# Attention block on one core: the lower part of V accumulated into the columns of its upper part

## The chip, the cores and the metric

The kernel runs on one core of one Trainium2 chip. The metric is the device time of one execution in microseconds (us); lower is better. Three timed runs of the kernel before gave 1442.44, 1429.75 and 1431.9 us, median 1431.9 us. A further execution was profiled, and all rows below come from it.

## The reference, cut to what matters

One block of a transformer: T = 1024 tokens, width 1024, a mixed attention of 8 dilated-window heads ("A") and 8 sparse heads in two groups ("B"), then an output projection and an MLP of width 4096. The change touches the place where probabilities meet V, in both halves:

```python
# A: three dilated windows, mixed by their denominators
e = jnp.where(mask, jnp.exp(s - m[..., None]), 0.0)
den = jnp.sum(e, axis=-1)
o = jnp.einsum('bhrnqk,bhrnkd->bhrnqd', e, vb.astype(jnp.float32)) / den[..., None]
...
# B: a selected and a sliding-window branch, gated and added to a compressed one
p_sel = masked_softmax(ss, (kpos <= tpos[:, None])[:, :, None])
o_sel = jnp.einsum('bgrqk,bgqkd->bgrqd', p_sel, vg.astype(f32))
...
p_win = masked_softmax(sw, wmask)
o_win = jnp.einsum('bgrqk,bgkd->bgrqd', p_win, vw.astype(f32))
out = gb[..., 0:1] * o_cmp + gb[..., 1:2] * o_sel + gb[..., 2:3] * o_win
...
h_res = h_res + mixed @ w_out[l]
h = rms_norm(h_res, norm_mlp[l])
h_res = h_res + jnp.square(jax.nn.relu(h @ w_up[l])) @ w_down[l]
```

## The kernel before, in words

Every float32 product is made of parts: a value is split into an upper part (a rounded copy) and a lower part (the rest), and upper times upper, upper times lower and lower times upper are summed in PSUM. The matmuls of projections, scores, output projection and MLP do so in fp32r. The product of probabilities and V does so in float16.

**V.** A tile of V has 130 float16 columns for each head and each block of 128 keys (L216). `split_v` (L200) puts the upper part into columns 64 to 127 and the lower part into columns 0 to 63; column 128 holds ones (L217) and yields the softmax denominator.

**One unit of attention** is one block of 128 queries, one head, and n blocks of 128 keys. `attend` (L503) runs it in steps:

- `st_scores` (L400): TensorE makes the scores (L417, L419, in B also a mask product, L421), VectorE adds mask or table and takes the extreme of a row (L428), for some units GpSimd adds a constant to that extreme (L432), ScalarE takes the exponential (L433).
- `st_trans` (L435): ScalarE writes the upper part of the probabilities in float16 (L447), GpSimd (L449) or VectorE (L451) writes the lower part, by turns D, P, P; one transposing DMA on SyncE's queue (L452) turns both into `pt`, with keys on the partitions. Units of at most 4 key blocks go through this step in pairs of two heads.
- `st_pv` (L457): for each key block t two matmuls. L467 takes the upper probabilities as weights and streams 129 columns of V (lower, upper, ones); L468 takes the lower probabilities as weights and streams 65 (upper, ones), added to columns 64 to 128. So a unit's result stands in PSUM as [product with V's lower part, 64 | all other products, 64 | denominator, 1]. Two heads lie side by side in one tile of tag `O`, 2 x 129 = 258 columns, and are evicted together after the second.

A unit's product is held back: it is issued one unit later in A (`DEPA`), three in B (`DEPB`).

**Eviction and the halves.** In A, VectorE copies the first 64 columns of both heads into `oaw` (L477), adds the next 64 from PSUM (L478), and copies the denominators (L479). When the four query blocks of a pair of heads are done, `done` (L609) divides (GpSimd, L613) and stores `oaw` to DRAM by SyncE's queue (L614). There is one buffer `oaw`, and while the A units run there is one PSUM bank of tag `O` (`nbank`, L342); from the second half of B's preparation on there are two. In B, ScalarE copies all 258 columns into the tile `ot` (L473, a tile of 8 heads x 129). After the eighth head `b_done` (L832) follows: VectorE scales and inverts the denominators (L835, L836), GpSimd multiplies them by the gate (L837), adds the two halves (L838), multiplies by the gated inverse (L839) and adds to the other branches (L840). After the second branch of a block, `finalize` (L845) squares the sum on ScalarE (L848, which writes its unneeded squares into columns 64 to 127 of `ot`) for the norm.

**Order of the work.** The list `P1` (L28) sets A's four pairs of heads, the projections and the compression of keys in turn, with projection matmuls between A's units. B then runs the query blocks in the order 5, 7, 6, 4, 3, 2, 1, 0 (`ORD`), the sliding window ahead of the selected blocks, with pieces of the output projection (L705) put in by a credit (`pump`, L857) and later jobs by a count (`waiting`). The MLP follows (L1042 ff.). The program is built by a framework that orders instructions by priority and a simulated timeline when it compiles, so each engine's order is fixed in the program; on the chip each engine runs its own list in order and waits on semaphores.

Of the kernel before, what the change touches and what calls it, by code (L numbers as in the profile page):

```python
# [9 lines left out]
F32 = mybir.dt.float32  # L10
# [3 lines left out]
AF = mybir.ActivationFunctionType  # L14
OP = mybir.AluOpType
# [41 lines left out]
def build(tc, A, out):  # L57
# [3 lines left out]
    pe, act, dve, pool, sp = nc.tensor, nc.scalar, nc.vector, nc.gpsimd, nc.sync  # L61
# [93 lines left out]
    vsc = cst.tile([128, 4], F32, name="vsc")  # L155
# [168 lines left out]
    oad = tc.dram_tile([NT, 128, 512], F32, name="oad")  # L324
# [21 lines left out]
    def bank(tag, shape, bufs=None):  # L346
        if tag == "F" and nbank[pst["second"]]["F"] == 0:
            tag = "O"
        n = nbank[pst["second"]][tag]
        p = pst["pool"] if tag in "OF" else psp  # L350
        t = p.tile([128, 512], F32, name=tag, tag=tag, bufs=n)
        if len(shape) == 3:
            return t[:, :shape[1] * shape[2]].rearrange("p (a b) -> p a b", a=shape[1])
        return t[:, :shape[1]]
# [7 lines left out]
    def k_stacks(ke, ko, srcs):  # L362
        n = len(srcs)
        ps = transposes(srcs)
        for e, o, i in zip(KS, (ke[0:64], ko[64:128]), (0, 64)):
            if e == "A":
                act.activation(o, ps[i:i + 64, :n], AF.Copy)
            else:
                dve.tensor_copy(o, ps[i:i + 64, :n])
        dve.tensor_sub(ke[64:128], ps[0:64, :n], f32(ke[0:64]))  # L370
        dve.tensor_sub(ko[0:64], ps[64:128, :n], f32(ko[64:128]))

    def q_stacks(qe, qo, q2, srcs):
        n = len(srcs)
        ps = transposes(srcs)
        for e, o, i in zip(QS, (qe[0:64], qo[64:128], qe[64:128], qo[0:64]), (0, 64, 0, 64)):
            if e == "A":
                act.activation(o, ps[i:i + 64, :n], AF.Copy, scale=0.125)
            else:
                dve.tensor_scalar(o, ps[i:i + 64, :n], 0.125, None, op0=OP.mult)  # L380
        dve.scalar_tensor_tensor(q2[0:64, 0], ps[0:64, :n], 0.125, f32(qe[0:64]), op0=OP.mult, op1=OP.subtract)
        dve.scalar_tensor_tensor(q2[64:128, 1], ps[64:128, :n], 0.125, f32(qo[64:128]), op0=OP.mult, op1=OP.subtract)
# [74 lines left out]
    def st_pv(u):  # L457
        n = u["n"]
        e = u["e"]
        if e == 0:  # L460
            OP2[0] = bank("O", [128, 258]).rearrange("p (a b) -> p a b", a=2)
        pss = OP2[0]
        ps = pss[:, e]
        for t in range(n):
            v = u["v"](t)
            ph, pl = u["pt"][t]
            pe.matmul(ps, ph, v[:, 0:129], start=t == 0, stop=False)  # L467
            pe.matmul(ps[:, 64:129], pl, v[:, 64:129], start=False, stop=t == n - 1)  # L468
        if e == 0:
            return  # L470
        if "ev" in u:
            if EV[u["h"] // 2] == "A":
                act.activation(u["ev"], pss, AF.Copy)  # L473
            else:
                dve.tensor_copy(u["ev"], pss)
        else:
            dve.tensor_copy(u["out"], pss[:, :, :64])  # L477
            dve.tensor_add(u["out"], u["out"], pss[:, :, 64:128])  # L478
            dve.tensor_copy(u["den"], pss[:, :, 128:129])  # L479

    OP2 = [None]
    pend = []
# [20 lines left out]
    def attend(u):  # L503
        st_scores(u)
        if paired(u) and not u["e"]:
            first[0] = u
        else:
            us = [first[0], u] if paired(u) else [u]
            st_trans(us)
            pend.append(us)  # L510
            retire(DEPB if "i" in u else DEPA)
        for job in waiting:
            job[0] -= 1
        due = [job for job in waiting if job[0] <= 0]
        waiting[:] = [job for job in waiting if job[0] > 0]
        for job in due:
            with later(0):
                pinned(u, job[1])
        if "i" in u:
            pump(u)  # L520
# [76 lines left out]
    def a_pair(hp):  # L597
        c = ("qk", hp)
        st = ST[c]
        k = asp.tile([128, 2, NT, 128], F32R, name="ak", bufs=1)  # L600
        for a in (0, 4):
            k_stacks(k[:, 0, a:a + 4], k[:, 1, a:a + 4], [st[:, t, 128:256] for t in range(a, a + 4)])
        for a in (4, 0):
            oaw = asp.tile([128, 4, 2, 64], F32, name="oaw", bufs=1)
            den = asp.tile([128, 4, 2], F32, name="dena", bufs=2)
            q = asp.tile([128, 2, 4, 128], F32R, name="aq", bufs=2)
            q2 = aq2
            q_stacks(q[:, 0], q[:, 1], q2, [st[:, t, 0:128] for t in range(a, a + 4)])
            def done(den=den, oaw=oaw, a=a):  # L609
                dve.tensor_scalar(den, den, vsc[:, hp // 2:hp // 2 + 1], None, op0=OP.mult)  # L610
                dve.reciprocal(den, den)
                o3 = oaw.rearrange("p t e d -> p (t e) d")
                pool.tensor_mul(o3, o3, den.rearrange("p t e -> p (t e)")[:, :, None].to_broadcast([128, 8, 64]))  # L613
                sp.dma_start(oad[a:a + 4, :, hp * 128:(hp + 1) * 128].rearrange("t p c -> p t c"),  # L614
                             oaw.rearrange("p t e d -> p t (e d)"))

            for i in range(3, -1, -1):
                for e in range(2):
                    u = dict(q=q[:, e, i], q2=q2[:, e, i], k=k[:, e].rearrange("p a b -> p (a b)"),
                             n=a + i + 1, tab=la[:, (7 - a - i) * 128:],  # L620
                             v=lambda t, e=e: V["a", hp][:, t, e], den=den[:, i, :, None], out=oaw[:, i], e=e)
                    if i == 0 and e == 1:
                        u["done"] = done
                    attend(u)
# [12 lines left out]
    ssm = cst.tile([128, 2, NT], F32, name="ssm")  # L637
# [82 lines left out]
    QB, OC, SB, OT, OB, DEN = {}, {}, {}, {}, {}, {}  # L720
# [3 lines left out]
    def fb(i, shape, dt, name, bufs):  # L724
        if name in FB:
            n = fbn[name] = fbn.get(name, -1) + 1
            if n % bufs == 0:
                return bqp.tile(shape, dt, name=name + "0", bufs=1)
            bufs -= 1
        return bpp.tile(shape, dt, name=name, bufs=bufs)  # L730
# [75 lines left out]
    def b_attend(i, br):  # L806
        n0 = max(0, i - 4)
        if br == 0:
            OB[i] = wop.tile([128, 8, 64], F32, name="ob", bufs=3)

        def f(br, h):
            g, j = divmod(h, 4)
            q, q2 = QB[i]
            if h == 0:
                OT[i, br] = fb(i, [128, 8, 129], F32, "ot", 2)
            k = kb[br][:, g].rearrange("p a b -> p (a b)")
            a, n = (0, i + 1) if br == 0 else (n0, i + 1 - n0)
            u = dict(i=i, h=h, q=q[:, g, j], q2=q2[:, g, j], k=k[:, a * 128:], n=n,
                     v=lambda t: V["kw" if br else "ks"][:, a + t, g], ev=OT[i, br][:, h - 1:h + 1], e=h % 2)
            if br:  # L820
                u["tab"] = wint[:, (5 - n) * 128:]
            else:
                u["sc"] = SB[i, g]
            return u

        for h in range(8):
            u = f(br, h)
            if h == 7:
                u["done"] = lambda: b_done(i, br)
            attend(u)  # L830

    def b_done(i, br):  # L832
        o = OT[i, br]
        d = DEN[i, br] = cst.tile([128, 8], F32, name="den", bufs=4)
        dve.tensor_scalar(d, o[:, :, 128], vsc[:, 2 + br:3 + br], None, op0=OP.mult)  # L835
        dve.reciprocal(d, d)  # L836
        pool.tensor_mul(d, d, gate[:, i].rearrange("p (h b) -> p b h", b=3)[:, 1 + br])  # L837
        pool.tensor_add(o[:, :, 0:64], o[:, :, 0:64], o[:, :, 64:128])  # L838
        pool.tensor_mul(o[:, :, 0:64], o[:, :, 0:64], d[:, :, None].to_broadcast([128, 8, 64]))  # L839
        pool.tensor_add(OC[i] if br else OB[i], o[:, :, 0:64], OC[i])  # L840
        if br == 0:
            finalize(i)
# [2 lines left out]

    def finalize(i):
        fin.add(i)
        act.activation(OT[i, 0][:, :, 64:128], OB[i], AF.Square, accum_out=ssm[:, 1, i:i + 1])  # L848
        rms_of(rmm[:, 1, i:i + 1], ssm[:, 1, i:i + 1], 512)

    pieces = []
# [240 lines left out]
    ps = [bank(x, [128, 512]) for x in "OF"]  # L1092
# [124 lines left out]
```

## Time and profile before

| | us |
|---|---|
| median of three runs | 1431.9 (1429.75 to 1442.44) |
| the profiled execution | 1436.43 |
| its span, first to last instruction | 1434.6 |
| TensorE matmul busy | 1356.6 (95%), 8267 matmuls |
| VectorE, ScalarE, GpSimd busy | 804.2, 620.4, 512.7 |
| mean granted TensorE clock | 0.976 of full |
| first and last product with V (L467, start) | 83.6 and 698.3 |

How to read the rows: PE is TensorE's matmuls, PEld its weight loads, DVE is VectorE, ACT ScalarE, POOL GpSimd, SP SyncE. "out<-in" names the tiles written and read. Matmuls are pipelined, so the duration of one (0.19 to 0.23 us for the products with V) is longer than its distance to the next; distances are read from the starts. In the table by windows each engine has its busy time in that stretch with the number of its instructions; after them come the granted clock, the busy share of the 16 DMA engines and the data rate. In the list of waits stands who waited for whom, the total, the number of times, and the longest. In the groups, "| 21.1, 1405 | 5.9 <-..." is busy time in us, mean of one in ns, and the engine's idle time just before the group with what ended it.

### The profile page before, as it was taken

What the parts mean: (1) busy time and instruction counts of PE and PEld (TensorE: products, weight loads), DVE (VectorE), ACT (ScalarE), POOL (GpSimd) and SP (SyncE); (2) the same over time, 40 slices, a digit from 0 to 9 for tenths busy, and PEclk for the clock granted to TensorE, in tenths of its full rate; (3) what the DMA queues carried; (4) which work ended last, traced back from release to release, by engine and by line L of the source; (5) the groups of instructions that cost most, each with busy time, mean ns of one, the idle gap of its engine ahead of it and who ended that gap; (6) DMA issues with size and microseconds to landing.
All of it is one profiled execution on the core that took longest, in us unless ns stands there. A gap on an engine that the chain in (4) does not pass through costs nothing.

```text
span 1434.6 us, 21829 instructions
## 1 busy us (share of the span) xinstructions
PE 1356.6 (95%) x8267; PEld 1150.8 (80%) x8267; DVE 804.2 (56%) x1728; ACT 620.4 (43%) x1092; POOL 512.7 (36%) x728
## 2 busy tenths in 40 slices
PE   8999999998978999899899999999999999999997
PEld 6898889998966777678678888888888888888886
DVE  6674656673467887877454434443354344443436
ACT  6572746763567777776472112211212112122115
POOL 3445564574466566877411111111111111111114
PEclk9999999999899999899999999999999999999998
DMA  5265563975558987765431111111112111111002
GB/s 186 67 127 132 100 139 70 227 153 135 93 148 167 159 155 138 141 118 103 111 111 30 59 45 59 46 41 47 45 59 59 44 30 46 58 59 45 1 0 118
DMA packets 285193, 131.55 MB, mean 92 GB/s; under 512 B 219040, under 2 KB 272288, under 8 KB 285088
## 3 DMA queue, kind: packets, MB, share of 16 engines
q1 hardware_dynamic: 284944, 129.90, 39.5%
q8 instruction: 65, 1.06, 0.3%
q14 instruction: 40, 0.33, 0.1%
q10 hardware_dynamic: 144, 0.26, 0.0%
HBM read 68.26 MB, written 8.39 MB: 53 GB/s over the span
## 4 chain that ended last, share of the span: by engine, by line
PE 65%; POOL 7%; DVE 7%; DMA 7%; issue 4%; ACT 4%; SPq 0%; POOLq 0%; DVEq 0%; ACTq 0%
PE dn L1056 8%; PE dn L1058 8%; PE dn L1057 8%; PE up L1024 8%; PE up L1022 8%; PE up L1023 8%; DMA pt<-hl 2%; PE F L334 2%; PE F L335 2%; PE F L336 2%; PE T L359 1%; DVE ns L428 1%; PE S L417 1%; POOL hl L449 1%; DMA pt<-hlx 1%
## 5 line engine op out<-in xcount | busy, mean ns | idle before, releaser
L1033 POOL TENSOR_TENSOR ul<-ua,uh 128x512 fp32r<-128x512 f32 x64 | 83.6, 1306 | 607.2 <-ACT uh L1032 527.7
L1059 DVE SCALAR_TENSOR_TENSOR st<-dn,r2q,st 128x512 f32<-128x512 f32 (+1 forms) x257 | 191.5, 746 | 155.9 <-PE dn L1058 152.4
L1056 PE MATMUL dn<-wdh,uh 128*128 128x512 f32 (+1 forms) x514 | 203.1, 395 | 0.0
L1058 PE MATMUL dn<-wdh,ul 128*128 128x512 f32 (+1 forms) x514 | 202.5, 394 | 0.0
L1057 PE MATMUL dn<-wdl,uh 128*128 128x512 f32 (+1 forms) x514 | 201.7, 392 | 0.0
L1022 PE MATMUL up<-h2h,wuh 128*128 128x512 f32 x480 | 187.8, 391 | 1.0 <-ACT wuh L94 1.0
L1024 PE MATMUL up<-h2h,wul 128*128 128x512 f32 x480 | 188.1, 392 | 0.5 <-DVE wul L95 0.5
L1023 PE MATMUL up<-h2l,wuh 128*128 128x512 f32 x480 | 187.3, 390 | 0.0
L334 PE MATMUL F<-wh,hh 128*128 128x256 f32 (+1 forms) x576 | 166.7, 291 | 3.6 <-ACT wh L94 2.2
L335 PE MATMUL F<-wl,hh 128*128 128x256 f32 (+1 forms) x576 | 165.8, 288 | 0.3 <-DVE wl L95 0.3
L336 PE MATMUL F<-wh,hl 128*128 128x256 f32 (+1 forms) x576 | 165.3, 287 | 0.0
L1030 ACT ACTIVATE ua<-up 128x512 f32<-128x512 f32 x60 | 35.2, 587 | 230.7 <-PE up L1024 230.7
L433 ACT ACTIVATE ns<-ns,mn 128x640 f32<-128x640 f32 (+7 forms) x152 | 110.2, 747 | 46.5 <-POOL mn L432 23.5
L467 PE MATMUL O<-v,pt 128*128 128x129 f16 x816 | 93.6, 227 | 30.0 <-DMA pt<-hl 19.4
L95 DVE TENSOR_TENSOR wul<-wur,wuh 128x1024 fp32r<-128x1024 f32 x32 | 39.4, 1232 | 134.9 <-ACT wuh L94 134.9
L1058 PEld LDWEIGHTS dn<-wdh,ul 128*128 128x128 f32 x514 | 96.9, 188 | 22.5
L334 PEld LDWEIGHTS F<-wh,hh 128*128 128x128 f32 x576 | 110.2, 192 | 5.7 <-ACT wh L94 3.1
L449 POOL TENSOR_TENSOR hl<-ns,hl 128x640 f16<-128x640 f32 (+5 forms) x67 | 104.4, 1560 | 27.5 <-ACT hl L447 21.6
L1057 PEld LDWEIGHTS dn<-wdl,uh 128*128 128x128 f32 x514 | 96.8, 188 | 21.6
L1056 PEld LDWEIGHTS dn<-wdh,uh 128*128 128x128 f32 x514 | 97.0, 189 | 21.0
L467 PEld LDWEIGHTS <-pt 128*128 128x128 f16 x816 | 74.1, 100 | 48.8 <-DMA pt<-hl 26.7
L335 PEld LDWEIGHTS F<-wl,hh 128*128 128x128 f32 x576 | 110.6, 192 | 1.1 <-DVE wl L95 0.6
(261 smaller groups left out, 3026.0 us busy)
## 6 DMA issues: line engine op xcount, KB each, us to landing
wur<-in_w_up_dram SPq DMA_DIRECT2D x32, 512.0 KB, 4.1
wdr<-in_w_down_dram SPq DMA_DIRECT2D x32, 512.0 KB, 4.0
wr<-in_w_in_dram SPq DMA_DIRECT2D x44, 256.0 KB, 3.0
st<-in_x_dram SPq DMA_DIRECT2D x8, 512.0 KB, 5.7
wor<-in_w_out_dram SPq DMA_DIRECT2D x16, 256.0 KB, 3.4
ns<-in_xT_dram SPq DMA_DIRECT2D x7, 512.0 KB, 5.5
out_dram<-st SPq DMA_DIRECT2D x7, 512.0 KB, 2.6
w<-in_w_k_dram SPq DMA_DIRECT2D x4, 512.0 KB, 5.1
```

What stands on the lines that cost most here:

```text
L334: pe.matmul(ps, hh[:, k, ts], hi, start=k == 0, stop=False)
L335: pe.matmul(ps, hh[:, k, ts], lo, start=False, stop=False)
L336: pe.matmul(ps, hl[:, k, ts], hi, start=False, stop=k == KD - 1)
L449: pool.tensor_sub(lo, p, hi)
L467: pe.matmul(ps, ph, v[:, 0:129], start=t == 0, stop=False)
L1022: pe.matmul(ps, hi[:, k], h2h[:, k, hs], start=k == 0, stop=False)
L1023: pe.matmul(ps, hi[:, k], h2l[:, k, hs], start=False, stop=False)
L1024: pe.matmul(ps, lo[:, k], h2h[:, k, hs], start=False, stop=k == KD - 1)
L1056: pe.matmul(ps, uh[:, ts], wh[:, cs], start=j == 0, stop=False)
L1057: pe.matmul(ps, uh[:, ts], wl[:, cs], start=False, stop=False)
L1058: pe.matmul(ps, ul[:, ts], wh[:, cs], start=False, stop=j == NB - 1)
L1059: dve.scalar_tensor_tensor(o[:, cs], ps, r2q[:, t:t + 1], o[:, cs], op0=OP.mult, op1=OP.add)
```

## The change

The products with V's lower part are added to the same 64 columns as all others. For this L467 becomes two matmuls with the same weights, one over the 65 columns of the upper part and the ones, one over the 64 columns of the lower part. A unit's result has 65 columns in PSUM, two heads 130; the additions of the two halves go (L478 in A, L838 in B), and the tile `ot` has 65 columns for each head. The square of `finalize` writes its unneeded values into columns 0 to 63 instead. Besides, the two lines of the store at L614 are joined into one, which is the same instruction.

```diff
@@ st_pv
         if e == 0:
-            OP2[0] = bank("O", [128, 258]).rearrange("p (a b) -> p a b", a=2)
+            OP2[0] = bank("O", [128, 130]).rearrange("p (a b) -> p a b", a=2)
         pss = OP2[0]
         ps = pss[:, e]
         for t in range(n):
             v = u["v"](t)
             ph, pl = u["pt"][t]
-            pe.matmul(ps, ph, v[:, 0:129], start=t == 0, stop=False)
-            pe.matmul(ps[:, 64:129], pl, v[:, 64:129], start=False, stop=t == n - 1)
+            pe.matmul(ps, ph, v[:, 64:129], start=t == 0, stop=False)
+            pe.matmul(ps[:, 0:64], ph, v[:, 0:64], start=False, stop=False)
+            pe.matmul(ps, pl, v[:, 64:129], start=False, stop=t == n - 1)
         if e == 0:
             return
         if "ev" in u:
...
         else:
-            dve.tensor_copy(u["out"], pss[:, :, :64])
-            dve.tensor_add(u["out"], u["out"], pss[:, :, 64:128])
-            dve.tensor_copy(u["den"], pss[:, :, 128:129])
+            dve.tensor_copy(u["out"], pss[:, :, 0:64])
+            dve.tensor_copy(u["den"], pss[:, :, 64:65])
@@ b_attend
-                OT[i, br] = fb(i, [128, 8, 129], F32, "ot", 2)
+                OT[i, br] = fb(i, [128, 8, 65], F32, "ot", 2)
@@ b_done
-        dve.tensor_scalar(d, o[:, :, 128], vsc[:, 2 + br:3 + br], None, op0=OP.mult)
+        dve.tensor_scalar(d, o[:, :, 64], vsc[:, 2 + br:3 + br], None, op0=OP.mult)
         dve.reciprocal(d, d)
         pool.tensor_mul(d, d, gate[:, i].rearrange("p (h b) -> p b h", b=3)[:, 1 + br])
-        pool.tensor_add(o[:, :, 0:64], o[:, :, 0:64], o[:, :, 64:128])
         pool.tensor_mul(o[:, :, 0:64], o[:, :, 0:64], d[:, :, None].to_broadcast([128, 8, 64]))
         pool.tensor_add(OC[i] if br else OB[i], o[:, :, 0:64], OC[i])
@@ finalize
-        act.activation(OT[i, 0][:, :, 64:128], OB[i], AF.Square, accum_out=ssm[:, 1, i:i + 1])
+        act.activation(OT[i, 0][:, :, 0:64], OB[i], AF.Square, accum_out=ssm[:, 1, i:i + 1])
```

More of the change, by code (lines that the diff above doesn't have):

```diff
@@ L613, in done @@
                 pool.tensor_mul(o3, o3, den.rearrange("p t e -> p (t e)")[:, :, None].to_broadcast([128, 8, 64]))
-                sp.dma_start(oad[a:a + 4, :, hp * 128:(hp + 1) * 128].rearrange("t p c -> p t c"),
-                             oaw.rearrange("p t e d -> p t (e d)"))
+                sp.dma_start(oad[a:a + 4, :, hp * 128:(hp + 1) * 128].rearrange("t p c -> p t c"), oaw.rearrange("p t e d -> p t (e d)"))
             for i in range(3, -1, -1):
```

## The prediction

> **What bounds the kernel now.** I read the page's totals first, then busy time by stage, then who waits for whom in the two stages that hold products with V.
>
> ```profile
> span 1434.6 us, 21829 instructions
> PE 1356.6 (95%) x8267; PEld 1150.8 (80%) x8267; DVE 804.2 (56%) x1728; ACT 620.4 (43%) x1092; POOL 512.7 (36%) x728
> ```
>
> ```profile
> core 0: us, PE busy (x) PEld busy (x) DVE busy (x) ACT busy (x) POOL busy (x), PEclk, DMA share, GB/s
> 83.00:345.00 262.00, 243.19 (x2151) 230.63 (x2149) 160.60 (x427) 148.23 (x294) 144.64 (x279) 0.97 0.65 141
> 371.00:699.00 328.00, 291.60 (x2344) 240.85 (x2342) 243.75 (x733) 227.44 (x409) 217.57 (x277) 0.93 0.72 136
> 708.00:1436.00 728.00, 715.76 (x3148) 586.41 (x3146) 326.24 (x431) 175.30 (x262) 97.93 (x79) 0.99 0.17 52
> ```
>
> The first two rows are A and B; from 708 us on there is the MLP, where TensorE is busy 98% and nothing of the change runs. In A TensorE is busy 93% (243.19 of 262), because projections fill the gaps. In B it is busy 89% (291.60 of 328), and four other resources stand between 66% and 74%: no single one bounds the stage, and what TensorE lacks are operands that come late through a long chain. The waits of B name them (engine, line, what it waited for; total, times, longest):
>
> ```profile
> ACT nsx L433 <- POOL mn L432: 22.0, 14, 3.1
> ...
> PEld L467 <- DMA pt<-hl: 19.3, 21, 3.3
> PEld S L417 <- DVE mn L428: 17.9, 27, 2.5
> ...
> PEld L467 <- DMA pt<-hlx: 6.3, 7, 2.1
> ```
>
> The three PEld rows are what TensorE misses: transposed probabilities (19.3 + 6.3) and a free bank for scores (17.9), 43.5 us together. The ACT row shows GpSimd as one cause: ScalarE's exponential waits 22.0 us for a one-column GpSimd instruction that stands behind long ones.
>
> **The products.** Each key block now has 3 pairs of weight load and matmul instead of 2; columns streamed are 65 + 64 + 65 = 194, as 129 + 65 = 194 were before. So the question is what one more pair costs. A burst of eight key blocks in TensorE's timeline (start, duration):
>
> ```profile
> 499.62 0.23 PE L467 MATMUL O<-v,pt 128*128 128x129 f16 x1 [0.75 <-DMA pt<-hlx]
> 499.69 0.19 PE L468 MATMUL O<-v,pt 128*128 128x65 f16 x1
> 499.72 0.22 PE L467 MATMUL O<-v,pt 128*128 128x129 f16 x1
> 499.78 0.19 PE L468 MATMUL O<-v,pt 128*128 128x65 f16 x1
> 499.81 0.22 PE L467 MATMUL O<-v,pt 128*128 128x129 f16 x1
> ...
> 500.31 0.19 PE L468 MATMUL O<-v,pt 128*128 128x65 f16 x1
> 500.33 0.42 PE L417 MATMUL S<-kb,qb 128*128 128x384 f32 x1
> ```
>
> Eight blocks take 500.33 - 499.62 = 0.71 us, 88.75 ns each. In each the wide matmul holds the array for 60 to 70 ns and the narrow one for about 29 (499.69 to 499.72, 499.78 to 499.81, with a grain of 10 ns). The weights of the next wide matmul are loaded in the shadow of the narrow one, so a load of 128 columns fits into some 29 ns:
>
> ```profile
> 499.78 0.10 PEld L467 LDWEIGHTS <-pt 128*128 128x128 f16 x1
> 499.81 0.10 PEld L468 LDWEIGHTS <-pt 128*128 128x128 f16 x1
> ```
>
> The load of L467 at 499.78 starts with the narrow matmul, and its own matmul starts at 499.81. Three narrow pairs at 29 ns are 87 ns, against 88.75 ns. The bounds of the added pair: below, three times 28 ns, 84 ns, 5 ns less per block; above, the front of TensorE may not keep up, since what the trace shows as sustained is 4 instructions in 88.75 ns, 22 ns each, so that 6 could need 133 ns, 44 ns more. How many blocks:
>
> ```profile
> L467 PE MATMUL O<-v,pt 128*128 128x129 f16 x816 | 93.6, 227 | 30.0 <-DMA pt<-hl 19.4 <-DVE dena L479 5.6 <-DMA pt<-hlx 5.0
> ```
>
> 816 blocks make -4 us to +36 us of TensorE, of which nine tenths count (93% and 89% busy above): -4 to +32 us. The nearest row is the narrow pair at 29 ns, measured with its load hidden, so I take about 1 ns more per block, **+1 us**; something has to be paid for a third start.
>
> The Trainium skill (TensorE: Matmul & The Clock Gate, section Back-to-back issue gap) says the opposite of this: in a sustained stream of load and matmul the spacing at 128 columns is about 81 ns, more than the columns need. By that, an added pair would cost up to 816 x 81 ns = 66 us. The trace does not agree: its pairs come at 88.75 / 2 = 44 ns, with 129 and 65 columns.
>
> **What is removed in A.** One VectorE instruction for two heads (group rows):
>
> ```profile
> L477 DVE COPY oaw<-O 128x128 f32<-128x128 f32 x32 | 9.2, 287 | 38.3 <-DMA oad<-oaw 20.0 <-PE O L468 18.2
> L478 DVE TENSOR_TENSOR oaw<-oaw,O 128x128 f32<-128x128 f32 x32 | 9.1, 284 | 0.6
> ```
>
> 32 times 284 ns are 9.1 us of VectorE, which is busy 61% of A (160.60 of 262). The copies beside it keep their sizes. With a single bank for products, TensorE waits for their end only sometimes:
>
> ```profile
> PE O L467 <- DVE dena L479: 5.6, 3, 3.3
> ```
>
> Three waits shrink by 0.28 us each, 0.9 us; the 20.0 us in which L477 waits for the store of `oaw` stay. If those waits are really made by the store, this is worth nothing; if all of the 9.1 us were on the path, 9.1. I take **-1 us**, because other work covers VectorE's remaining saving.
>
> **What is removed in B.** Rows of that stage alone:
>
> ```profile
> L473 ACT ACTIVATE ot<-O 128x258 f32<-128x258 f32 x64 | 24.0, 380 | 29.8 <-PE O L468 29.4
> ...
> L838 POOL TENSOR_TENSOR ot<-ot 128x512 f32<-128x512 f32 x15 | 21.1, 1405 | 5.9 <-ACT ot L473 5.5
> ...
> L835 DVE TENSOR_SCALAR den<-ot,vsc 128x8 f32<-128x8 f32 x15 | 10.7, 710 | 4.7 <-ACT ot L473 4.6
> ...
> L702 ACT ACTIVATE mh<-T 128x512 fp32r<-128x512 f32 x15 | 8.8, 588 | 1.9 <-PE T L359 1.8
> ...
> L837 POOL TENSOR_TENSOR den<-den,gate 128x8 f32<-128x8 f32 x15 | 4.8, 319 | 2.0 <-DVE den L836 1.6
> ```
>
> GpSimd loses L838: 15 x 1405 ns = 21.1 us, 9.7% of its 217.57 us. ScalarE's eviction goes from 258 to 130 columns: from the PSUM reads of 512 and 258 columns, (588 - 380) / 254 = 0.82 ns a column, so about 105 ns less, 64 times, 6.7 us (2.9% of 227.44). VectorE's L835 works on 8 columns and yet takes 710 ns on average, while its shortest is 193:
>
> ```profile
> L835 DVE TENSOR_SCALAR den<-ot,vsc x16: 193/716/1252, 406.2 to 699.2; 128x8 f32<-128x8 f32 x16
> ```
>
> It is long when it runs beside L838, as the end of B shows below; without it, up to 15 x 517 ns = 7.8 us of VectorE go (3.2% of 243.75).
>
> How much of this reaches TensorE? Its waits of 43.5 us come from all three engines and from DMAs. Cut by the mean of 9.7, 3.2 and 2.9% they lose 2.3 us; cut by GpSimd's share, 4.2 us. Against that stands a wait that moves: L837 hardly waits today (2.0 us over 15), since L838 runs while VectorE makes the reciprocal. Afterwards L837 is first in GpSimd's list of that job and waits in its place, with L839, L840 and whatever L432 and L449 stand behind it. That can give back at most what L838 took, so the lower end is 0, and the upper end is 21 us if GpSimd alone paced B. I take **-3 us**, near the cut by shares, since GpSimd is busy only 66% of the stage.
>
> **The end of B.** Here the chain is short and its steps can be read one by one (timeline; L836, L837, L839 and L840 follow between the second row and the last):
>
> ```profile
> 699.08 1.29 POOL L838 TENSOR_TENSOR ot<-ot 128x512 f32<-128x512 f32 x1 [3.02 <-ACT ot L473]
> 699.17 1.23 DVE L835 TENSOR_SCALAR den<-ot,vsc 128x8 f32<-128x8 f32 x1
> ...
> 703.37 0.66 PE L359 MATMUL T<-c_ident,ob 128*128 128x128 f32 x4 [1.04 <-POOL ob L840]
> ```
>
> L835 lasts as long as L838 beside it, and everything after hangs on it. At 0.2 us it ends 1.0 us sooner, and the eviction ahead is 0.1 us shorter; TensorE idles 1.04 us for this chain, so **-1 us**, bounded by that idle time.
>
> **Sum.** +1 - 1 - 3 - 1 = -4 us. The profiled execution took 1436.4 us (span plus 1.8), so its like would be 1432.4; it stood 4.5 us above the median of 1431.9, from which the forecast is **1428 us**, 0.3% less. About 1%, 14 us, is what a measurement of this kernel can tell from no change. The instructions' order is set again when the program is compiled; that moves single waits of 1 to 3 us in either direction, and I put it into the range.
>
> **Rivals.**
>
> - *GpSimd paced B all along.* For it: ScalarE's 22.0 us for L432. Against: 66% busy, and two of the three TensorE waits are for DMAs. Then all 21.1 us go, with the -1 of A and the +1 of the products: about 1411 us. Chance 0.18.
> - *TensorE's front can't feed three short pairs.* Each pair costs 44 ns as the mean of today's two does, a block takes 133 ns: +32 us, less the savings of 5: 1459 us. It makes the kernel slower by 1% from (14 + 5) / (0.9 x 816) = 26 ns more per block on, that is from 115 ns. For it: no burst of the trace has two narrow pairs in a row. Against: the narrow pair stands at 29 ns with its load in it. Chance 0.12, in which cases between 115 and 133 ns are counted.
> - *The wait only moves.* L837 takes L838's place on GpSimd, and a new order costs what the rest gains: 1432 us, no change. For it: the engines are all below 75% in B, so shorter work there may only lengthen idle time. Chance 0.15.
>
> The forecast itself has 0.55, with its own range 1420 to 1436. The range reaches down to 1409, so that it takes in the first rival's time, and up to 1447, which is the second at some 27 ns more per block (1432 - 4 + 19); what lies beyond on either side is about 0.15. Faster by over 1% is the first rival and little beside, 0.19; slower by over 1% is the second with a bad order, 0.14; within 1% the rest, 0.67.
>
> **What would show it.** Right, if a burst of products has starts about 29 ns apart and a key block stays within 84 to 92 ns; L835 falls to 0.2 to 0.4 us; L473 to about 275 ns; L838 and L478 are gone; L837 shows an idle time before it of some 0.3 to 1 us each; B is 2 to 5 us shorter and the MLP the same. Wrong, if a block takes over 115 ns, if B shortens by 15 us or more, or if TensorE's waits for `pt` grow although GpSimd has less to do.

## The result

| | before | after |
|---|---|---|
| median of 10 runs each | 1431.8 us (1428.4 to 1442.4) | 1447.2 us (1442.4 to 1456.5) |
| ratio | | 1.010 (95%: 1.0078 to 1.0122) |
| the profiled execution | 1436.4 us, span 1434.6 | 1456.5 us, span 1454.7 |

The kernel became 1.0% slower, some 15 us. The forecast was 1428 us with a range up to 1447, so the time lies at, and by 0.2 us beyond, the range's upper end. It got there by a way that no rival had with this price. The profiled execution of the kernel after is the slowest of its ten, 9 us over their median, and that of before stands 5 us over its own. Two of 113 executions of the kernel before that were timed beside the experiments took 2648 and 4326 us, and no ratio here counts them. In the profile of the kernel after, L467, L468 and L469 are the three products; from the eviction on (L474 for L473), through `load_wo` and `out_proj`, every line number is off by one or two: L669 is the rounding of a weight piece (L670 before), L710 to L712 are the output projection (L711 to L713), L714 its result's eviction (L715), L834 the scaling of the denominators (L835), L836 the gate (L837).

The page's totals after:

```profile
span 1454.7 us, 23456 instructions
...
PE 1371.4 (94%) x9083; PEld 1167.0 (80%) x9083; DVE 791.2 (54%) x1696; ACT 615.7 (42%) x1092; POOL 490.0 (34%) x712
```

TensorE has 816 matmuls more, VectorE, ScalarE and GpSimd have less to do, as the diff says. Next the stretches that were read before, and B alone, from its first to its last `b_done` (the columns are those of the prediction's table; the second row is cut at 699 us as there, although B now ends later):

```profile
83.00:345.00 262.00, 245.92 (x2423) 233.01 (x2423) 158.63 (x404) 149.08 (x289) 144.00 (x279) 0.96 0.67 139
371.00:699.00 328.00, 289.97 (x2746) 243.95 (x2745) 231.13 (x705) 215.84 (x385) 188.99 (x247) 0.90 0.68 130
...
410.60:720.00 309.40, 267.94 (x2541) 220.22 (x2541) 224.49 (x680) 208.24 (x376) 183.92 (x219) 0.89 0.71 138
```

The same stretch of the kernel before, first to last `b_done`:

```profile
406.00:699.00 293.00, 257.16 (x2053) 207.06 (x2053) 230.43 (x680) 213.72 (x376) 203.05 (x233) 0.94 0.75 145
```

B's loop takes 309.4 us where it took 293.0, 16.4 us more. Ahead of it lie 4.6 us more (410.6 against 406.0), behind it 0.9 us less (1454.7 - 720.0 against 1434.6 - 699.0): 16.4 of the profiled difference of 20.1 us lie in B. GpSimd is busy 19 us less in a loop that lasts 16 us longer. TensorE stands idle 41.5 us in it, where it stood 35.8, and is busy 10.8 us more, at a granted clock of 0.89 against 0.94.

The pieces that the prediction wanted to see are nearly all there. The burst (timeline, start and duration) and rows of B after (groups of B, then L834 with its minimum, median and maximum):

```profile
502.51 0.20 PE L467 MATMUL O<-v,pt 128*128 128x65 f16 x1 [0.93 <-DMA pt<-hlx]
502.55 0.20 PE L468 MATMUL O<-v,pt 128*128 128x64 f16 x1
502.58 0.19 PE L469 MATMUL O<-v,pt 128*128 128x65 f16 x1
502.61 0.19 PE L467 MATMUL O<-v,pt 128*128 128x65 f16 x1
...
503.16 0.19 PE L467 MATMUL O<-v,pt 128*128 128x65 f16 x1
```

```profile
L474 ACT ACTIVATE ot<-O 128x130 f32<-128x130 f32 x64 | 17.3, 274 | 39.1 <-PE O L469 38.5
...
L836 POOL TENSOR_TENSOR den<-den,gate 128x8 f32<-128x8 f32 x15 | 4.2, 282 | 10.5 <-DVE den L835 8.2 <-DVE csc L797 1.8
```

```profile
L834 DVE TENSOR_SCALAR den<-ot,vsc x16: 214/231/1229, 410.9 to 720.1; 128x8 f32<-128x8 f32 x16
```

Seven key blocks last from 502.51 to 503.16, 92.9 ns each; over all bursts at full clock, from one block's first start to the next one's, it is 92.9 ns, against 88.7 before. The eviction lasts 274 ns (forecast 275), the median of the denominators' scaling is 231 ns, and the gate waits 10.5 us over 15 times, 0.7 us each (forecast 0.3 to 1). And yet B is longer. What waits there (from the list of waits between 371 and 720 us):

```profile
ACT nsx L433 <- POOL mn L432: 22.8, 17, 3.8
...
PEld L467 <- DMA pt<-hl: 15.4, 15, 3.0
ACT woh L669 <- DVE wor L668: 12.3, 5, 4.4
...
PEld S L417 <- DVE mn L428: 10.5, 15, 2.8
...
PEld F L710 <- DVE st L714: 6.3, 3, 4.0
PEld F L710 <- ACT woh L669: 5.2, 3, 2.1
```

The waits on which the prediction built became shorter (the longer of the two for transposed probabilities 19.3 to 15.4, the bank for scores 17.9 to 10.5). Others became long that the diff doesn't touch: the output projection's, for its bank and its rounded weights. The lists of the engines stand in another order than before. By the lists used below, the longest sequence that both orders share has 7099 of TensorE's 8187 matmuls, 1158 of VectorE's 1424 instructions, 844 of ScalarE's 1019 and 587 of GpSimd's 724, and TensorE's first difference comes at 85 us, in A.

### The profile page after: what moved, and what is told of

The parts are those of the page before. It is cut to its first block, busy times and chain, and to the rows that moved or that the text cites. A ratio compares the mean times of both kernels' runs of the same rounds, so it can differ in the third digit from the quotient of the medians.

```text
span 1454.7 us, 23456 instructions
## 1 busy us (share of the span) xinstructions
PE 1371.4 (94%) x9083; PEld 1167.0 (80%) x9083; DVE 791.2 (54%) x1696; ACT 615.7 (42%) x1092; POOL 490.0 (34%) x712
## 4 chain that ended last, share of the span: by engine, by line
PE 72%; DVE 8%; DMA 6%; POOL 5%; issue 5%; ACT 2%; SPq 0%; POOLq 0%; DVEq 0%; ACTq 0%
PE dn L1054 8%; PE dn L1056 8%; PE dn L1055 8%; PE up L1022 8%; PE up L1020 8%; PE up L1021 7%; PE F L334 3%; PE F L335 3%; PE F L336 3%; DMA pt<-hl 3%; PE S L417 2%; PE T L359 2%; PE S L419 2%; DVE ns L428 1%; PE F L710 1%
## 5 line engine op out<-in xcount | busy, mean ns | idle before, releaser
L433 ACT ACTIVATE ns<-ns,mn 128x640 f32<-128x640 f32 (+7 forms) x152 | 110.7, 747 | 40.3 <-POOL mn L432 23.9
L467 PE MATMUL O<-v,pt 128*128 128x65 f16 x816 | 94.9, 199 | 24.5 <-DMA pt<-hl 15.7
L449 POOL TENSOR_TENSOR hl<-ns,hl 128x640 f16<-128x640 f32 (+5 forms) x67 | 105.8, 1580 | 35.1 <-ACT hl L447 28.8
L336 PEld LDWEIGHTS F<-wh,hl 128*128 128x128 f32 x576 | 111.8, 194 | 0.5
```

Of the source, the lines that this page charges most:

```text
L336: pe.matmul(ps, hl[:, k, ts], hi, start=False, stop=k == KD - 1)
L433: u["exp"] = act.activation(ns[:, :n * 128], ns[:, :n * 128], AF.Exp, scale=-1.0, bias=mn[:, j:j + 1])
L449: pool.tensor_sub(lo, p, hi)
```

## The experiments

**Theories.** O: what costs is the new order that the compiler set, above all in B's loop. W: the work itself costs, three pairs per key block or the wait that moves. To tell them apart, a kernel's instructions were held to an order given as a list: an edge without any wait or semaphore between each instruction and the next one on its engine, so that the compiler cannot set another. That holding an order costs little by itself is seen in one pair: the kernel after took 1447.2 us, and 1446.1 when held to the same order (with two more weight buffers). Each kernel below was timed 4 to 12 times, beside the kernel before; a cost in us beside a ratio is the ratio's excess over 1, times the 1431 to 1434 us of before. Where such a list is used the diff is one line, with the function behind it:

```diff
         build(tc, aps, o[0])
+        queue_as(tc, ORDER)
```
```python
for queue in traced.values():          # the instructions of one engine as written
    mine, places = places[:len(queue)], places[len(queue):]
    for a, b in zip(mine, mine[1:]):
        tc.add_manual_dep(queue[b], queue[a].name, how, reason="order")
```

**Work and order crossed.** The kernel after in the order of before (a key block's two upper products stand where L467 stood; a removed instruction leaves no place):

> The changed kernel, every instruction of it, but each engine's list stands in the order of the kernel before (edges of issue order alone, no waits; what the change adds or drops is put in or left out in place). Theory O (the new order, which the compiler's simulated timeline chose, is what costs the 15 us, and the changed work itself is worth what was forecast): 1423 to 1432 us, not slower than before, with some 60 to 80 us at half clock. Theory W (the work costs it: three short pairs per key block feed TensorE worse, or lower its clock): 1442 to 1452 us, as the changed kernel, with some 100 us at half clock.

The kernel before in the order of after:

> The kernel before, every instruction of it, in the order that the changed kernel's lists have (the additions of the halves stand behind the instruction that they followed). Theory O: 1442 to 1455 us, slower by 1% or more than before, with more time at half clock. Theory W: 1428 to 1436 us, as before.

Measured: the new work in the old order 1436.6 us, ratio 1.0027 (1.0004 to 1.0050), 3.9 us over before; the old work in the new order 1452.4 us, ratio 1.013 (1.0091 to 1.017), 18.6 us over. So the order alone, without a single instruction changed, costs as much as the whole change and more, and W is left with a few us. The 1436.6 us are 5 us above what O gave the work in the old order (1423 to 1432) and below W's 1442. In the new order the new work is the faster one (1447.2 against 1452.4 us, ratios 1.010 and 1.013, whose intervals overlap), so what the work is worth may itself depend on the order. The loops from first to last `b_done`, first of the new work in the old order, then of the old work in the new order:

```profile
410.80:704.00 293.20, 260.89 (x2541) 213.07 (x2541) 223.55 (x680) 208.55 (x376) 182.72 (x218) 0.92 0.75 145
```

```profile
404.30:714.60 310.30, 262.94 (x2053) 212.69 (x2053) 231.62 (x680) 213.66 (x376) 203.81 (x233) 0.91 0.69 136
```

The second row is to be read against that of before: the same 2053 matmuls, 680, 376 and 233 instructions, the busy times of VectorE, ScalarE and GpSimd equal within 1.2 us, and 310.3 us in place of 293.0. TensorE is idle 47.4 us (310.30 - 262.94), 11.5 us more, and busy 5.8 us more at a lower clock.

**The change's two halves, in the old order.** The split alone (L467 in two, additions and evictions as before), and the shorter eviction with the additions gone but without the split:

```diff
# e3: the split alone
-            pe.matmul(ps, ph, v[:, 0:129], start=t == 0, stop=False)
+            pe.matmul(ps[:, 64:129], ph, v[:, 64:129], start=t == 0, stop=False)
+            pe.matmul(ps[:, 0:64], ph, v[:, 0:64], start=False, stop=False)
# e4: the shorter eviction alone
-                act.activation(u["ev"], pss, AF.Copy)
+                act.activation(u["ev"], pss[:, :, 64:129], AF.Copy)
...
-        pool.tensor_add(o[:, :, 0:64], o[:, :, 0:64], o[:, :, 64:128])
```

> The product's split alone, in the order of the kernel before: three short pairs per key block, but the lower part's product still goes to its own 64 columns, with 129 columns per head, the wide eviction and the additions as before. Theory O: the split costs 0 to 4 us, so 1430 to 1436 us. Theory W, if the third pair is the cost: 1442 us or more.

> The eviction alone, in the order of the kernel before: the two matmuls of before into 129 columns, but only 65 columns per head are evicted, into the small tile, and nothing is added; the product with V's lower part is computed and left out of the output. Theory O and the forecast: 3 to 8 us faster than before, 1424 to 1429 us. Theory W, if shorter eviction and fewer additions make a wait somewhere else: 1432 us or more.

Measured: the split 1437.8 us, ratio 1.003 (1.0005 to 1.0054), 4.3 us; the eviction 1433.7 us, ratio 1.0007 (0.9982 to 1.0031), nothing. The second leaves the product with V's lower part out of the result. The 4.2 ns more per key block make 816 x 4.2 = 3.4 us, which is the split's cost within its interval. The 5 us that the eviction and the additions were to bring aren't there: its interval reaches down to -2.6 us, and 1433.7 us lie where the expectation put theory W for this half (1432 or more).

**Where the order costs.** The kernel before with B's loop in its old order and all else in the new one, and the reverse:

> The kernel before, every instruction; what is traced in the loop over query blocks (B's loop) stands in the old order, everything ahead of it in the order of the changed kernel. Theory B (the new order loses its time in B's loop, where it places instructions that wait for a late operand ahead of ready ones; the new order of A loses nothing): 1427 to 1437 us, as before. Theory A (the order of A and of the change from A to B, and the buffers and queues it leaves behind, cost it): 1445 us or more.

> The reverse: the kernel before, every instruction; B's loop in the order of the changed kernel, everything ahead of it in the old order. Theory B: 1445 to 1456 us, all of the loss. Theory A: 1427 to 1437 us.

Measured: 1432.7 us, ratio 0.9993 (0.9968 to 1.0018), and 1450.3 us, ratio 1.0102 (1.0067 to 1.0136). The loss is in B's loop, all of it as far as the intervals tell (10 to 19 us, against 13 to 24 with the whole new order); the other order in A and in the projections ahead of it costs nothing that can be seen. Then B's loop cut in two at the job of its sixth branch:

> The kernel before, its work unchanged; only the instructions of B's loop up to the job of the sixth of 16 branches (the stretch that ends near 550 us) stand in the order of the kernel after, all others in their old order. The run with the new order in the whole loop took 1450.3 us, some 17 us more than the kernel before; its starts of L835 fell behind those of before by 6 us up to the cut and by 11 us behind it. Theory M (many waits, each small, spread over the loop): +5 to +7 us, 1437 to 1440 us, and together with the run that has the new order behind the cut the two excesses add up to 15 to 19 us. Theory P (one place in the lists sets off all the rest): one of the two runs shows nearly the whole excess, the other stays within 2 us of the kernel before.

> The kernel before, its work unchanged; the instructions of B's loop behind that cut (query blocks' branches 6 to 16) stand in the order of the kernel after, all others in their old order. Theory M: +10 to +12 us, 1443 to 1446 us. Theory P: either nearly all 17 us (1449 or more) or at most 2 us over the kernel before (1435 or less).

Measured: 1444.1 us (1.0078, 1.0050 to 1.0106) and 1443.5 us (1.0074, 1.0044 to 1.0104), 11 us each. The first was expected lower, so the lag of the denominators' starts isn't a good measure of what a part costs in the end. The two add up to 22 us, against 15 with the whole loop (17 by the medians). Each part costs by itself: there is no single place from which all the rest follows.

**Which waits.** Three waits before (beside those in the prediction), then the list with the old work in the new order, both between 404 and 716 us:

```profile
ACT ot L848 <- POOL ob L840: 5.3, 2, 4.3
...
ACT woh L670 <- DVE wor L669: 2.9, 3, 1.4
PEld F L711 <- DVE st L715: 2.9, 7, 0.9
```

```profile
ACT nsx L433 <- POOL mn L432: 27.4, 18, 4.9
...
ACT woh L670 <- DVE wor L669: 11.7, 5, 4.3
...
ACT ot L848 <- POOL ob L840: 9.3, 6, 3.6
...
POOL den L837 <- DVE den L836: 8.2, 7, 2.3
PEld F L711 <- DVE st L715: 8.2, 4, 4.2
```

Beside waits inside the attention (L433 for L432, and GpSimd's L449 for L447, from 6.0 to 13.5 us), those grew that stand between engines at the pieces of other jobs that stand inside the attention's lists: weights of the output projection to be rounded, its bank to be emptied, the norm's square. (The 5.3 us of the square before lie almost whole, 4.3 us, behind the loop.) One such place in the timeline of the old work in the new order:

```profile
594.47 0.33 SPq L658 DMA_DIRECT2D wor<-in_w_out_dram  x1
...
597.32 1.36 DVE L669 TENSOR_SCALAR wor<-wor,gvec 128x512 f32<-128x512 f32 x1 [4.76 <-DMA wor<-in_w_out_dram]
598.60 0.81 DVE L451 SCALAR_TENSOR_TENSOR hl<-ns,hl 128x640 f16<-128x640 f32 x1
...
599.45 0.75 DVE L715 SCALAR_TENSOR_TENSOR st<-F,rmm,st 128x512 f32<-128x512 f32 x1
...
600.25 0.79 PE L711 MATMUL F<-woh,mh 128*128 128x512 f32 x1 [3.63 <-DVE st L715]
```

The load of a weight piece is issued at 594.47, VectorE stands at L669 until 597.32, and the eviction L715 is two instructions behind it in VectorE's list; TensorE stands at L711 until 600.25. From this place a theory was made (L): the late weight pieces hold VectorE and so the projection's bank. It was tried twice. First with four buffers for a loaded piece in the kernel after, its own order kept:

```diff
-            raw = bpp.tile([128, 512], F32, name="wor", bufs=2)
+            raw = bpp.tile([128, 512], F32, name="wor", bufs=4)
```

> The changed kernel in its own order, with 4 buffers instead of 2 for the raw pieces of the output projection's weights, so that a piece's transfer need not wait until an earlier piece is split. Theory B1 (the loss in B is mainly VectorE waiting, at the head of its list, for such a late transfer, with the eviction of the output projection behind it): 4 to 8 us faster than the changed kernel, 1439 to 1443 us. Rival (many small waits of this kind, none of them more than a fraction): 1445 to 1450 us, as the changed kernel.

Measured: 1446.1 us, ratio 1.007 (1.0046 to 1.0093), 1 us under the kernel after by the medians and 4 by the ratios (1.007 and 1.010, with intervals that overlap); 4 to 8 were expected if theory L held. In its trace VectorE still waits 5.3 us for three of these loads (5.6 in the kernel after): a missing buffer wasn't what made them late. Then without the loads at all, in both orders (the projection multiplies by pieces of the identity matrix in place of its weights):

```diff
-            sp.dma_start(raw, A["w_out"][k * 128:(k + 1) * 128, cs])
...
-                    dve.tensor_scalar(raw, raw, g, None, op0=OP.mult)
+                    dve.tensor_scalar(raw.rearrange("p (a b) -> p a b", a=4), ident[:, None, :].to_broadcast([128, 4, 128]), g, None, op0=OP.mult)
```

> The kernel before in the order of the kernel after throughout (1452.4 us as it stands), without the sixteen loads of w_out: L669 reads the identity matrix instead of the loaded piece, so the output projection multiplies by identity blocks. No instruction of VectorE waits for these transfers any more, and SyncE's queue has sixteen entries fewer; all lists are otherwise as they were. Theory L (the late weight pieces hold up VectorE, and the evictions of F behind them): 1440 us or less, at least 10 us of the 20 gone, and TensorE's waits for L715 fall from 15 us to below 6. Theory M (the lists themselves; the transfer is only the last of many to end a wait): 1446 to 1453.

> The control: the kernel before in its own order, without the sixteen loads of w_out (L669 reads the identity matrix). In its trace L669 waits little for the transfers, so both theories expect 1430 to 1433 us, the same as the kernel before; what it gains is to be taken off the gain of the run in the new order.

Measured: 1450.9 us in the new order (1.0118, 1.0067 to 1.0169) and 1430.3 us in the old one (0.9954, 0.9925 to 0.9982). By the medians the order costs 21.3 us with the loads (1452.4 against 1431.2 of the kernel before beside it) and 20.5 us without them (1450.9 - 1430.3); by the ratios it is 18.6 and 23.5. At least 10 us were to go by L, so L falls. Waits in the new order without the loads (its lines are one lower than before's):

```profile
ACT woh L669 <- DVE wor L668: 9.6, 4, 4.3
...
PEld F L710 <- DVE st L714: 7.0, 5, 2.7
```

No transfer is left to wait for, and most of the waits stay (11.7 to 9.6, 8.2 to 7.0): the load was only what ended one of them last.

**Is it the split that brings a costly order about?** The order that each kernel gets when it is compiled by itself was timed for five more: the eviction alone, the split alone, the kernel after held to the order of the eviction's kernel, the kernel after with four and with three weight buffers, and the kernel before with three buffers for the extremes (`mn`, L411) in place of four.

> The eviction alone again (two matmuls into 129 columns, 65 evicted, nothing added, the lower part's product left out of the output), now in the order that the compiler chooses for it by itself. Theory O says that each such order is a draw of its own: it may stand anywhere from 1425 to 1455 us, and lies more than 4 us from the same work in the old order (1433.7 us). If the new order's loss came from the changed work's nature instead, this kernel with work as in the old order would stand within 4 us of it.

> The split into three products per key block and its smaller results, as in the kernel after, but with the columns of V in their old places (65 columns from 64 on, accumulated there); the order is the one that the program gets when this kernel is compiled by itself. The same work in the order of the kernel before took 1437.8 us. Theory T (three matmuls per key block make the compiler set an order that costs B's loop its time): 1445 us or more. Theory D (each compilation sets another order, most of them good, and the kernel after got a costly one): 1434 to 1441.

(The text on record of the split speaks of smaller results; the kernel that ran has the split and nothing else, its results have 129 columns and the additions are there, as in the split above.)

> The kernel after, its work unchanged, in the order that the kernel with the shorter eviction alone (1433.6 us in that order) got when it was compiled. The kernel after took 1447.2 us in its own order and 1436.6 in the order of the kernel before. Theory D (its own order is the costly thing): 1433 to 1440 us in this third order too. Rival (any order made for other work costs, or none but the old one suits the three products): 1443 us or more.

> The kernel after with four buffers for the loaded pieces of w_out in place of two, in the order that it gets when compiled so. The same work in the order of the kernel after took 1446.1 us. Theory T (the split itself leads the compiler to a costly order each time): 1443 us or more, as in both orders compiled with the split so far. Theory D (a draw, good or bad): it may as well come out at 1433 to 1440.

> The kernel after with three buffers for the loaded pieces of w_out, in the order that it gets when compiled so: one more order compiled with the split. Theory T: 1443 us or more. Theory D: it may as well come out at 1433 to 1440.

> The kernel before with three buffers in place of four for the extremes of the rows (mn), in the order that it gets when compiled so: a third order compiled without the split. Theory T (only orders compiled with the split cost B's loop its time): 1430 to 1437 us. Theory D: it may as well come out at 1443 or more. The missing buffer by itself may add waits, so a slow result would not by itself speak for theory D.

| kernel | order | us | ratio to before (95%) |
|---|---|---|---|
| eviction alone | its own | 1433.6 | 1.0004 (0.9976 to 1.0032) |
| split alone | its own | 1449.2 | 1.0115 (1.0083 to 1.0147) |
| after | the eviction kernel's | 1435.1 | 1.0009 (0.9984 to 1.0034) |
| after, four weight buffers | its own | 1441.0 | 1.0048 (1.0017 to 1.0079) |
| after, three weight buffers | its own | 1432.6 | 1.0003 (0.9976 to 1.0029) |
| before, three `mn` | its own | 1441.3 | 1.0073 (1.0042 to 1.0104) |

The first row fell into the rival's range: by theory O the eviction's own order was to lie more than 4 us from the same work in the old one, and it lies at 1433.6 against 1433.7. After the first two rows it looked as if the split led the compiler astray. The row with three weight buffers speaks against that: an order compiled with the split is good (1432.6). The other two rows fell between the ranges expected: 1441.0 with four buffers, and 1441.3 for an order compiled without the split, where the missing buffer may have a part. The kernel after alone, its work unchanged, stands at 1447.2, 1436.6 and 1435.1 us in three orders; how often a compilation sets a costly one, seven orders can't tell. The loops of the kernel after in its third order and of the one with three weight buffers:

```profile
404.60:692.00 287.40, 255.42 (x2541) 209.93 (x2541) 224.78 (x680) 208.38 (x376) 184.02 (x218) 0.94 0.76 147
```

```profile
401.20:692.60 291.40, 258.62 (x2542) 212.27 (x2543) 235.08 (x680) 206.45 (x376) 184.02 (x218) 0.94 0.75 143
```

287.4 and 291.4 us for the work that takes the kernel after 309.4. These are single executions, and the first is the fastest of its ten where that of the kernel after is the slowest: the medians of these two differ by 12 us, not 22. None of these versions is measurably faster than the kernel before.

## Why the prediction was wrong, step by step

- **The order** is the step that failed: it was put at single waits that may go either way, and so at nothing in the sum. The prediction said: "The instructions' order is set again when the program is compiled; that moves single waits of 1 to 3 us in either direction, and I put it into the range". The runs show 18.6 us (13 to 24 by the interval 1.0091 to 1.017) for the order of the kernel after with the work of before, in B's loop as far as the intervals tell. There TensorE is idle 11.5 us more and busy 5.8 us more at a lower clock, and the lists show many waits of up to 5.6 us, whose growth does not cancel. The rival "The wait only moves" had the words "a new order costs what the rest gains", and a price of 4 us: the cause was named and mis-sized by a factor of four to five. Its chance of 0.15 ended at 1432.
- **The products**: forecast +1 us, measured 4.3 us for the split alone in the old order. The block is 92.9 ns, not 89 to 90; the bounds (-4 to +32) held, and TensorE's front feeds three short pairs, at 31 ns a start. The range's upper end, 1447 us, was that rival with some 27 ns more per block; that the measured time stands beside it is chance, for a block has 4 ns more.
- **A and B's removed work**: forecast -1, -3 and -1. The instructions became shorter as forecast (eviction 274 ns, scaling 231 ns, GpSimd 19 us less), but the shorter eviction and the missing additions alone gave 1.0007 (0.9982 to 1.0031). Part of it may be given back by a lower clock (below); that was not tried. Also, the 43.5 us that the prediction took as TensorE's loss are waits of weight loads, part of which pass beside running matmuls: by its own table the matmuls stood idle 36.4 us in that stretch (328.00 - 291.60). GpSimd did not pace B: that rival (1411 us) is out.
- **The end of B**: L834 there lasts 0.22 us, as forecast; a gain of 1 us is below what can be seen.
- **The sum** with a fair order: the new work stands at 1436.6, 1435.1 and 1432.6 us in three orders other than its own (the last with a third weight buffer), 0 to 4 us above before by the ratios, where the forecast had 4 us below. So in these orders the kernel stands inside the forecast's own range of 1420 to 1436, or at its edge, but with no change, and not with the gain that was forecast. The signs named for a wrong forecast did not point to it: no block over 115 ns, no shorter B, and waits for `pt` that fell.

What stays open: which property of an order makes it costly. The loss was cut by stretches of the loop, but not by engine, so which engine's list costs isn't known. Nor is it known how much of the loss the lower clock makes and how much the waits.

## What to carry to other kernels

Where a compiler sets the order of the engines' lists anew for each program, a small edit can be timed together with a new draw of that order; before a gain or loss of about 1% is put down to the edit, run the old work in the new order and the new work in the old one. In a forecast for such a kernel the spread of orders is a term with a size of its own, measured by compiling harmless variants, and not a few single waits. A long wait found in the profile of a slow order is a candidate and no cause: take the resource away and see whether the time goes with it.

## What the runs showed of the chip

- **Run time goes with TensorE's granted clock.** Over 111 runs of the kernel before the fastest took 1425.4 us at a mean granted clock of 0.984 and the slowest 1443.0 us at 0.974; a line through them falls by 1.2 us per 0.001 of clock. In the profiled executions the clock is granted at 1 or at 0.5, and at 0.5 for 70.8 us before, 109.8 after, 90.9 with the new work in the old order and 78.3 with the old work in the new one (the first experiment expected 60 to 80 by theory O, some 100 by theory W). The median clock of the runs is 0.981 before, 0.970 after, 0.974 with the new work in the old order and 0.974 with the old work in the new one. At 0.974 the line gives 1441 us: the new work in the old order stands 5 us under it, the old work in the new order 11 us over it. So a lower clock goes with the new work as well as with the new order, and may hide what the removed instructions bring. In B's loop the kernel after has 0.89 where the kernel before has 0.94, and more of its loss lies in slower matmuls (10.8 us) than in idle TensorE (5.7 us), though part of the busy time is the third product. Whether the idle gaps or the work bring the lower clock about isn't shown.
- **Three short pairs cost little more than two pairs with the same columns**: 92.9 ns against 88.7. The Trainium skill (TensorE: Matmul & The Clock Gate, section Back-to-back issue gap) gives about 81 ns for each matmul in a stream of load and matmul at 128 columns. The traces here have 59 ns for a pair at 129 columns (before) and 31 ns at 64 and 65 columns (after), and the measurement decides.
- **L835 is long when it runs beside a long GpSimd instruction.** In the trace before nine of its 16 instances take over 0.6 us, and L838 runs beside eight of them, L449 beside the ninth. With L838 gone and the old order kept, its median falls from 716 to 226 ns (L834, first row). With L838 still there, but in the order of after, it is 232 ns (second row), and the three instances over 0.6 us run beside L671, L449 and L840. In both of these traces and in that of the kernel after, none that runs alone takes over 0.24 us.

```profile
L834 DVE TENSOR_SCALAR den<-ot,vsc x16: 199/226/1392, 411.0 to 704.2; 128x8 f32<-128x8 f32 x16
```

```profile
L835 DVE TENSOR_SCALAR den<-ot,vsc x16: 219/232/1229, 404.5 to 714.9; 128x8 f32<-128x8 f32 x16
```

So the prediction read rightly what made it long, but a new order shortens it as well, and the instances grow long again beside other GpSimd work (1392 ns at most without L838).
